# Delta rule in a hybrid encoder layer: q and k left as the convolution gives them, their norms applied as factors elsewhere

## The chip, the core and the metric

The kernel runs on one core of a Trainium2 chip. The core has TensorE (PE, matmuls and transposes into PSUM), VectorE (DVE), ScalarE (ACT), GpSimd (POOL) and SyncE (SP, which issues most of the DMAs). The metric is the time of one execution on the device in microseconds (us), lower is better. All data are float32; a large product is made of three matmuls of a rounded part and a remainder (hi x lo, lo x hi, hi x hi).

## The reference, cut to what matters

One encoder layer for two sequences, a prompt of 1024 tokens and a sample of 256, with 1024 features each: an input projection, two groups of heads side by side (four gated delta-rule heads, four differential-attention heads), an output projection, a layer norm, a SwiGLU block, a layer norm. The part that the change touches is the delta rule, which runs forward and backward in chunks:

```python
def l2norm(t, eps=1e-6):
    return t * lax.rsqrt(jnp.sum(t * t, -1, keepdims=True) + eps)

def delta_rule_chunked(q, k, v, g, beta):
    ...
    m = jnp.where(strict, jnp.einsum('bhnid,bhnjd->bhnij', kb, k) * decay, 0.0)   # kb = k * beta
    a_mat = m + jnp.eye(CHUNK, dtype=jnp.float32)
    sol = lax.linalg.triangular_solve(a_mat, rhs, ...)     # rhs: v * beta and kb * exp(gc)
    attn = jnp.einsum('bhnid,bhnjd->bhnij', q, k) * decay
    ...
    def step(state, xs):
        v_new = u_c - jnp.einsum('bhcd,bhde->bhce', w_c, state)
        o = jnp.einsum('bhcd,bhde->bhce', qd_c, state) + jnp.einsum('bhij,bhje->bhie', attn_c, v_new)
        state = state * gl_c[..., None, None] + jnp.einsum('bhcd,bhce->bhde', kd_c, v_new)

def gated_deltanet_group(qkv, z, gates, conv_w, a_log, dt_bias, norm_g):
    c = jax.nn.silu(centred_depthwise_conv(qkv, conv_w))   # 5 taps
    q, k, v = jnp.split(c, ...)
    q = l2norm(q) * (GDN_DK ** -0.5)                        # 128 features a head
    k = l2norm(k)
    ...
    o = rms_norm(o_f + o_b, norm_g) * jax.nn.silu(z)
```

## The kernel before, in words

The kernel has three stages that matter here, one behind the other. A scheduler (the program is built with a timeline model) fixes each engine's order from the order in which the code issues its instructions, with priorities; on the chip every engine works its list in that order.

**phase_a** (L592) is the input projection. `dense_T` (L175) takes up to three columns of 128 weights at a time: it loads them, splits them into hi (ACT) and lo (DVE, L163), and runs three matmuls for each of eight parts of the depth over the three token blocks (two of 512, one of 256; xh, xl are the split input; dps is the PSUM tile). After each half of a product over 512 tokens it calls `advance()` (L651), which takes one step in each of three lines of work for the delta rule: `fronts`, `blocks_` and `levels`. There are five such preparations, one for each of the four heads of the prompt and one for the sample with all of its heads. The last three columns (LAST) go through `dense_T` together; the third pair of weights, whl, borrows a buffer from the preparation.

A preparation starts from `conv_silu` (L322): five taps on DVE and a Silu on ACT, in a layout with the features on the partitions. `prep_front` (L340) transposes q, k and v on PE (nat_ps, L352) so that the tokens lie on the partitions, copies them on ACT (L355 q and k into raw, L358 v), squares them (L362), sums (L363), takes the inverse root (`rsqrt_small` L310, the power on POOL, L315), and multiplies raw by it on DVE (L371, 128x2048). `prep_group` (L385), two for each preparation with four chunks of 128 tokens each, transposes raw back (t_ps, L397), copies that on ACT into kqT (L398), writes kqT to the record rec in DRAM (L399), forms the decay factors, the products k k and k q (kq_ps, L430), and from them N, the blocks to be inverted, and more parts of the record. `invert_blocks` (L462) inverts the diagonal blocks in rows of 16 and 32 on DVE (tiles Wb, Ub, itmp, iT, iR), `spread_blocks` (L508) sends the result through DRAM into the tile UD (ublk, L512 to L517), and `invert_levels` (L526) puts the blocks together on PE: inv_ps from (UD, N) with 32x32, from (UD, Z) and (Z, UD), then the same with 64x64, with copies on ACT and DVE between them and a product with nbeta (L575) on DVE, and writes UD to rec (L578).

Two PSUM buffers of the tag tp serve all these transposes. `rope` (L750) turns the attention's q and k in the last columns' time.

**phase_b** (L1080) runs the attention and the delta rule's chunks. The attention makes 40 score tiles: s_ps (L839, L840), a maximum on DVE (L841), the exponential on ACT (L843, ap), transposes (tt_ps), the product with v, and the query steps before them (L799 to L806). Two threads of `chain` (L978) go through the chunks beside it: `chain_load` (L965) reads three tiles ld of a chunk from rec, and the first matmul of a chunk is vn_ps (L1027). `chain_finish` (L1057) squares a head's output (L1064), sums on DVE (L1066), and scales it. After that come the output projection, the layer norm and the SwiGLU block, which PE bounds and the change does not touch.

## Time and profile before

| | us |
|---|---|
| median of three runs | 1757.56 (1757.21 to 1760.45) |
| the profiled execution, its own time | 1751.05 |
| its span, first to last instruction | 1749.3 |
| projection with its preparations (phase_a) | 0 to about 509 |
| attention and chunks (phase_b) | 509 to about 801 |
| output projection to the end | 801 to 1749.3 |
| PE busy in the span | 1694.2 (97%) |
| DVE, ACT, POOL busy | 1191.9 (68%), 777.5 (44%), 213.1 (12%) |

The busy share of an engine is a mean over stages. Times in the rows are from the start of the span. The granted clock of PE is given as a share of its full speed of 2.4 GHz; 0.50 is its lower level, 1.2 GHz. The length of a matmul in the trace is from its start to its modelled end, and they overlap; how much of PE one takes is read from the distance of the starts.

### The profile page before, as it was taken

The numbers are of one execution on the slowest core, as the hardware profiler recorded it, in microseconds if no ns is written. First come the engines' busy times: TensorE is split into PE (matmuls) and PEld (weight loads), VectorE is DVE, ScalarE is ACT, GpSimd is POOL, SyncE is SP. The second block draws the span as 40 slices with busy tenths as digits, with TensorE's granted clock in tenths as the row PEclk, the third lists the DMA queues.
The fourth block names the chain that finished last, engine by engine and source line by source line (L and its number), as shares of the span: only waits on it lengthen the run. The fifth ranks groups of instructions, "written<-read, shape, count | busy, mean of one in ns | idle before, by whom it ended". The sixth has DMA issues, their size and how long they took to land.

```text
span 1749.3 us, 27337 instructions
## 1 busy us (share of the span) xinstructions
PE 1694.2 (97%) x10234; PEld 1471.2 (84%) x10234; DVE 1191.9 (68%) x2114; ACT 777.5 (44%) x1518; POOL 213.1 (12%) x197
## 2 busy tenths in 40 slices
PE   8999999999988999999999999999999999999998
PEld 8898888888867998788888888888888887888886
DVE  4635968878575589885676866556656665666696
ACT  4457486564337677775114322222222223543330
POOL 1000000000014445532330000000000000000011
PEclk9999999999988999999999999999999999999999
DMA  6234265676667996516521544333333524975541
GB/s 219 65 100 115 75 164 176 155 207 168 184 172 218 280 266 200 173 51 223 159 96 43 191 149 149 111 128 131 116 136 125 175 99 138 391 254 172 174 158 72
DMA packets 253554, 279.02 MB, mean 160 GB/s; under 512 B 47713, under 2 KB 198127, under 8 KB 252015
## 3 DMA queue, kind: packets, MB, share of 16 engines
q1 hardware_dynamic: 243519, 265.19, 48.5%
q10 hardware_dynamic: 9904, 12.10, 2.0%
q8 instruction: 80, 1.31, 0.3%
q14 instruction: 51, 0.42, 0.1%
HBM read 183.80 MB, written 93.43 MB: 158 GB/s over the span
## 4 chain that ended last, share of the span: by engine, by line
PE 54%; DMA 1%; ACT 1%; DVE 1%; issue 1%; POOLq 0%; POOL 0%; DVEq 0%; SPq 0%; ACTq 0%
PE dn_ps L1507 15%; PE gy_ps L1281 9%; PE gs_ps L1281 7%; PE gx_ps L1281 6%; PE gz_ps L1281 6%; PE om_ps L172 6%; PE gp_ps L1281 3%; DMA worw<-in_w_out_dram 1%; PE o_ps L879 1%; PE x_ps L1186 0%; ACT ap L843 0%; PE s_ps L839 0%; ACT woh L1166 0%; PE s_ps L840 0%; PE tt_ps L866 0%
## 5 line engine op out<-in xcount | busy, mean ns | idle before, releaser
L1297 ACT CAST sph<-wraw 128x512 fp32r<-128x512 f32 x92 | 57.0, 623 | 195.4 <-PE gy_ps L1281 124.4
L315 POOL TENSOR_TENSOR rs_r<-lva,mhalf 128x1 f32<-128x1 f32 x20 | 29.5, 1475 | 835.5 <-DVE lva L1143 817.1
L172 PE MATMUL dps<-xh,whi 128*128 128x512 f32 (+1 forms) x552 | 126.1, 363 | 0.0
L172 PE MATMUL dps<-xh,wlo 128*128 128x512 f32 (+1 forms) x552 | 124.5, 360 | 0.0
L172 PE MATMUL dps<-xl,whi 128*128 128x512 f32 (+1 forms) x552 | 123.4, 363 | 0.0
L1297 ACT CAST sph<-wsum 128x512 fp32r<-128x512 f32 x80 | 49.8, 622 | 156.6 <-PE gy_ps L1281 48.8
L1507 PE MATMUL dn_ps<-tth,ssh 128*128 128x512 f32 x280 | 108.9, 389 | 0.0
L1507 PE MATMUL dn_ps<-ttl,ssh 128*128 128x512 f32 x280 | 108.8, 389 | 0.0
L1507 PE MATMUL dn_ps<-tth,ssl 128*128 128x512 f32 x280 | 108.1, 389 | 0.0
L172 PEld LDWEIGHTS dps<-xh,wlo 128*128 128x128 f32 x552 | 94.8, 191 | 14.8
L172 PEld LDWEIGHTS dps<-xl,whi 128*128 128x128 f32 x552 | 94.2, 193 | 15.4
L172 PEld LDWEIGHTS dps<-xh,whi 128*128 128x128 f32 x552 | 94.5, 191 | 14.6
L841 DVE TENSOR_REDUCE ast<-s_ps 128x1 f32<-128x1024 f32 (+1 forms) x80 | 83.5, 1056 | 21.7 <-PE s_ps L840 19.6
L1298 DVE TENSOR_TENSOR spl<-wraw,sph 128x512 fp32r<-128x512 f32 x92 | 63.0, 687 | 48.2 <-PE gs_ps L1281 29.9
L334 DVE SCALAR_TENSOR_TENSOR c<-pad,cw,c 128x1024 f32<-128x1024 f32 (+1 forms) x96 | 82.1, 884 | 17.1 <-ACT c L332 16.6
L843 ACT ACTIVATE ap<-s_ps,ast 128x1024 f32<-128x1024 f32 (+1 forms) x80 | 80.0, 1001 | 29.4 <-DVE ast L841 29.1
L1298 DVE TENSOR_TENSOR spl<-wsum,sph 128x512 fp32r<-128x512 f32 x80 | 55.0, 688 | 46.6 <-issue 20.4
L1498 ACT CAST ssh<-sraw 128x640 fp32r<-128x640 f32 x77 | 56.0, 727 | 47.6 <-PE dn_ps L1507 34.3
L1499 DVE TENSOR_TENSOR ssl<-sraw,ssh 128x640 fp32r<-128x640 f32 x77 | 63.1, 820 | 16.8 <-ACT ssh L1498 13.1
L839 PE MATMUL s_ps<-akl,aq 128*128 128x512 f32 (+1 forms) x144 | 63.7, 444 | 7.7 <-ACT ap L843 7.6
L855 POOL TENSOR_TENSOR ap<-ap,ap 128x512 f32<-128x512 f32 (+2 forms) x60 | 63.0, 1069 | 64.6 <-ACT ap L852 31.6
L879 PE MATMUL o_ps<-av,tt 128*128 128x128 f32 x544 | 64.2, 275 | 0.0
(398 smaller groups left out, 4258.9 us busy)
## 6 DMA issues: line engine op xcount, KB each, us to landing
ld<-rec SPq DMA_DIRECT2D x160, 192.0 KB, 4.2
sraw<-hs SPq DMA_DIRECT2D x77, 320.0 KB, 4.3
wraw<-in_w_gate_up_dram SPq DMA_DIRECT2D x22, 1024.0 KB, 5.7
wraw<-in_w_in_dram SPq DMA_DIRECT2D x26, 512.0 KB, 4.5
wdraw<-in_w_down_dram SPq DMA_DIRECT2D x11, 1024.0 KB, 5.1
ws<-wdraw SPq DMA_DIRECT2D x11, 1024.0 KB, 3.9
traw<-ws SPq DMA_DIRECT2D x44, 256.0 KB, 4.5
araw<-dqk SPq DMA_DIRECT2D x40, 256.0 KB, 5.4
```

Of the source, the lines that this page charges most:

```text
L172: nc.tensor.matmul(out, lhsT=a(i), rhs=b(i), start=start and j == 0, stop=stop and j == len(seq) - 1)
L334: V.scalar_tensor_tensor(out=out, in0=pad[:, so + w:so + w + n], scalar=k.cw[:, w * 12 + ti:w * 12 + ti + 1], in1=out, op0=ALU.mult, op1=A ...
L839: nc.tensor.matmul(ps[:, o:o + w], lhsT=a.q[m][:, qs], rhs=a.kl[m][:, k0 + o:k0 + o + w], start=True, stop=False)
L841: V.tensor_reduce(out=st[:, m:m + 1], in_=ps, op=ALU.max, axis=AX.X, negate=True)
L843: A.activation(p, ps, AF.Exp, bias=st[:, m:m + 1], accum_out=a.s0[:, i:i + 1] if m == 0 else st[:, 2:3])
L855: nc.gpsimd.tensor_tensor(out=pr[0][:, c], in0=pr[0][:, c], in1=pr[1][:, c], op=ALU.add)
L879: nc.tensor.matmul(ps[:, j * P:(j + 1) * P], lhsT=tt[:, i, j * P:(j + 1) * P], rhs=a.v[:, v0 + i, :], start=i == 0, stop=i == NT[a.si] - 1)
L1281: m = nc.tensor.matmul(ps, lhsT=a(i), rhs=b(i), start=start and j == 0, stop=stop and j == len(seq) - 1, skip_group_check=again)
L1297: A.copy(hi, src)
L1298: V.tensor_tensor(out=lo, in0=src, in1=f32(hi), op=ALU.subtract)
L1499: V.tensor_tensor(out=lo, in0=src, in1=f32(hi), op=ALU.subtract)
L1507: nc.tensor.matmul(ps, lhsT=a[:, c], rhs=b, start=z == 0 and j == 0, stop=z == NPR - 1 and j == 2)
```

## The change

q and k stay as the convolution's Silu leaves them, features on the partitions, in one tile kqT of 128 x 2 x 1024 (two buffers in turn, by head), which is written to the record directly and is the operand of kq_ps. The transposes back and the copies behind them are gone, and so is the scaling of raw, which now holds k alone. Both are still transposed once, for their norms: the squares are read from PSUM. The inverse norm of k becomes factors: its square goes into nbeta and ekd in place, and it multiplies v on the way out of PSUM (vn, now on DVE). The inverse norm of q is kept as rq, and comes into `chain_finish` as the scale of the Square, which is now one activation for each 128 tokens with a sum of its own (eight for a prompt head, two for one of the sample), and once more in the factor of the output. The record has one axis of eight chunks rather than two of four. The flag that lets the next head's convolution go on is set behind vn; a second flag, all, is set behind the groups, and the buffers of kqT wait for it. The third weights of the last projection columns take a buffer of kqT, and the code waits for the sample's groups before it issues these columns. rope takes the other one.

```diff
 dense_T
-            hl = k.gp1.tile([P, 2, KT, P], F32R, tag=("raw", "wx")[len(W) - 2], name="whl")
+            hl = k.gp1.tile([P, 2, KT, P], F32R, tag="kqT0", name="whl")
 ...
 prep_front
-    raw = gp.tile([P, 2, 8, P], F32, tag="raw", name="raw")
+    raw = gp.tile([P, 8, P], F32, tag="raw", name="raw")
+    for s in range(2):
+        nc.sync.dma_start(out=rec[:, :, 3 + s, :], in_=kq[:, s].rearrange("p (u c) -> p u c", u=8))
     for g in range(2):
         u0 = 4 * g
-        for role in (0, 1, 2):
+        sq = gp.tile([P, 12, P], F32, tag="kq", name="sq")[:, 0:8]
+        for s in range(2):
             ps = k.pt.tile([P, 512], F32, tag="tp", name="nat_ps")
             for i in range(4):
-                nc.tensor.transpose(ps[:, i * P:(i + 1) * P], c3[role][:, (u0 + i) * P:(u0 + i + 1) * P], k.ident)
+                nc.tensor.transpose(ps[:, i * P:(i + 1) * P], kq[:, s, (u0 + i) * P:(u0 + i + 1) * P], k.ident)
             pv = ps.rearrange("p (a b) -> p a b", a=4)
-            if role < 2:
-                A.copy(raw[:, role, u0:u0 + 4], pv)
-            else:
-                vn = gp.tile([P, 4, P], F32, tag="kv", name="vn")
-                A.copy(vn, pv)
-                nc.sync.dma_start(out=k.S.rec[si][vh][g][:, :, 5, :], in_=vn)
-        sq = gp.tile([P, 12, P], F32, tag="kq", name="sq")[:, 0:8]
-        for role in range(2):
-            A.activation(sq[:, 4 * role:4 * role + 4], raw[:, role, u0:u0 + 4], AF.Square)
+            A.activation(sq[:, 4 * s:4 * s + 4], pv, AF.Square)
+            if s == 0:
+                A.copy(raw[:, u0:u0 + 4], pv)
         V.tensor_reduce(out=ss[:, :, u0:u0 + 4], in_=sq.rearrange("p (a b) c -> p a b c", a=2), op=ALU.add, axis=AX.X)
         yield
-    flag.done = True
     ...
+    inv = gp.tile([P, 8], F32, tag="l2i", name="l2i")
+    V.reciprocal(out=inv, in_=ss[:, 0])
+    nb = view(G.nbeta, o0, [[nt8, 2], [1, 8]])
+    V.tensor_tensor(out=nb, in0=nb, in1=inv.unsqueeze(1).to_broadcast([P, 2, 8]), op=ALU.mult)
+    ek = G.ekd[:, o0:o0 + 8]
+    V.tensor_tensor(out=ek, in0=ek, in1=inv, op=ALU.mult)
     rs = rsqrt_small(k, sf, 16, gp, "l2")
-    V.tensor_scalar(out=rs[:, 0:8], in0=rs[:, 0:8], scalar1=P ** -0.5, scalar2=None, op0=ALU.mult)
-    rv = raw.rearrange("p a b c -> p (a b) c")
-    V.tensor_tensor(out=rv, in0=rv, in1=rs.unsqueeze(2).to_broadcast([P, 16, P]), op=ALU.mult)
-    yield
+    V.tensor_tensor(out=inv, in0=ss[:, 0], in1=rs[:, 0:8], op=ALU.mult)
+    V.tensor_scalar(out=G.rq[:, o0:o0 + 8], in0=rs[:, 8:16], scalar1=P ** -0.5, scalar2=None, op0=ALU.mult)
+    for g in range(2):
+        ...
+            nc.tensor.transpose(ps[:, i * P:(i + 1) * P], vT[:, (u0 + i) * P:(u0 + i + 1) * P], k.ident)
+        vn = gp.tile([P, 4, P], F32, tag="kv", name="vn")
+        V.tensor_tensor(out=vn, in0=ps.rearrange("p (a b) -> p a b", a=4),
+                        in1=inv[:, u0:u0 + 4].unsqueeze(2).to_broadcast([P, 4, P]), op=ALU.mult)
+        nc.sync.dma_start(out=rec[:, u0:u0 + 4, 5, :], in_=vn)
+    flag.done = True
     yield
 ...
 prep_group
-    kqT = gp.tile([P, 4, 2, P], F32, tag="kqT", name="kqT")
-    for role in range(2):
-        ps = k.pt.tile([P, 512], F32, tag="tp", name="t_ps")
-        for i in range(4):
-            nc.tensor.transpose(ps[:, i * P:(i + 1) * P], raw[:, role, u0 + i, :], k.ident)
-        A.copy(kqT[:, :, 1 - role, :], ps.rearrange("p (a b) -> p a b", a=4))
-    nc.sync.dma_start(out=rec[:, :, 3:5, :], in_=kqT)
 ...
 invert_levels
-    for g in range(2):
-        for d, res in ((0, U), (1, Db)):
-            nc.sync.dma_start(out=k.S.rec[si][vh][g][:, :, 6 * d, :], in_=res[:, 4 * g:4 * g + 4, :])
+    for d, res in ((0, U), (1, Db)):
+        nc.sync.dma_start(out=k.S.rec[si][vh][:, :, 6 * d, :], in_=res)
 ...
 phase_a
-                            wait(flag)
-                            c3.append(conv_silu(k, 1, role, h, pad))
+                            if role == 0:
+                                wait(past, "all")
+                                out.kq = conv_out(h)
+                            elif role == 2:
+                                wait(flag)
+                                out.v = k.gp1.tile([P, 1024], F32, tag="c2", name="vT")
+                            conv_silu(k, 1, role, h, pad, (out.kq[:, 1], out.kq[:, 0], getattr(out, "v", None))[role])
 ...
             elif i == len(rest) - LAST:
+                wait(flag, "all")
                 dense_T(k, rest[i:], advance)
 ...
 rope
-        x = k.gp1.tile([P, 4, n], F32, tag=f"c{j % 2}", name="rx")
+        x = both[:, j % 2]
 ...
 chain_finish
-    A.activation(sv, o, AF.Square)
     ss = k.cf.tile([P, 8], F32, tag="css", name="css")[:, :nt]
-    V.tensor_reduce(out=ss, in_=sv, op=ALU.add, axis=AX.X)
+    rq = k.G[si].rq[:, h * nt:(h + 1) * nt]
+    for c in range(nt):
+        A.activation(sv[:, c], o[:, c], AF.Square, scale=rq[:, c:c + 1], accum_out=ss[:, c:c + 1])
     V.tensor_scalar(out=ss, in0=ss, scalar1=1.0 / P, scalar2=1e-6, op0=ALU.mult, op1=ALU.add)
     r = rsqrt_small(k, ss, nt, k.cf, "crms")
+    V.tensor_tensor(out=r, in0=r, in1=rq, op=ALU.mult)
```

The order of PE in the projection, where the preparation of the prompt's second head stands among the matmuls (dps). Before:

```order
L397 MATMUL t_ps<-identr,raw 128x128 x4
L172 MATMUL dps<-xh_153,whi 128x512
L172 MATMUL dps<-xh_283,whi 128x256
L172 MATMUL dps<-xh_153,whi 128x512
L172 MATMUL dps<-xh_283,whi 128x256
L536 MATMUL inv_ps<-UD_773,N 32x32 x32
L430 MATMUL kq_ps<-kqT 128x256 x4
L397 MATMUL t_ps<-identr,raw 128x128 x4
```

And now:

```order
L380 MATMUL nat_ps<-identr,vT 128x128 x8
L172 MATMUL dps<-xl_284,whi 128x256 x3
L172 MATMUL dps<-xh_283,wlo 128x256 x8
L172 MATMUL dps<-xh_283,whi 128x256 x8
L437 MATMUL kq_ps<-kqT 128x256 x4
L172 MATMUL dps<-xl_154,whi 128x512 x8
```

t_ps is gone, v's transposes stand by themselves behind those of q and k, and kq_ps follows without a transpose of its own.

The order of PE at the seam of the projection and the attention, where the sample's 32x32 groups (inv_ps) stand. Before:

```order
L172 MATMUL dps<-xl_284,whl 128x256 x8
L172 MATMUL dps<-xh_283,whl 128x256 x16
L839 MATMUL s_ps<-akl,aq 128x512
L840 MATMUL s_ps<-akh,aq 128x512
...
L536 MATMUL inv_ps<-UD_773,N 32x32 x32
L839 MATMUL s_ps<-akl,aq 128x512
L840 MATMUL s_ps<-akh,aq 128x512
...
L536 MATMUL inv_ps<-UD_772,Z 32x32 x8
```

And now:

```order
L172 MATMUL dps<-xl_284,whi 128x256 x8
L172 MATMUL dps<-xh_283,wlo 128x256 x4
L543 MATMUL inv_ps<-UD_775,N 32x32 x32
L172 MATMUL dps<-xh_283,wlo 128x256 x4
L172 MATMUL dps<-xh_283,whi 128x256 x8
L172 MATMUL dps<-xl_284,whi 128x256 x8
L172 MATMUL dps<-xh_283,wlo 128x256 x8
L172 MATMUL dps<-xh_283,whi 128x256 x4
L543 MATMUL inv_ps<-UD_774,Z 32x32 x8
```

The groups stood behind the first eight and twelve score matmuls; now they stand between the last 256-column matmuls of the projection, with 60 of these behind the first of them. The first vn_ps stands behind 40 score matmuls before, behind 28 now.

The order of DVE where the sample's inversion (Ub, itmp, iT from Wb) begins, near the end of the projection. Before:

```order
L163 TENSOR_TENSOR wlo<-wraw,whi 128x1024
L770 TENSOR_TENSOR rx<-rx 128x256
L163 TENSOR_TENSOR whl<-wraw,whl 128x1024
L478 COPY Ub<-Wb 128x16
L474 TENSOR_TENSOR itmp<-Wb,Ub 128x32
```

And now:

```order
L520 COPY itmp<-Ub 64x1024
L485 COPY Ub<-Wb 128x16
L481 TENSOR_TENSOR itmp<-Wb,Ub 128x32
L782 TENSOR_TENSOR rx<-rx,rcs 128x256
L482 TENSOR_REDUCE iT<-itmp 128x16
L783 TENSOR_TENSOR rx<-rx,rcs 128x256
L784 TENSOR_TENSOR rx<-rx,rcs 128x256
L481 TENSOR_TENSOR itmp<-Wb,Ub 128x32
L785 TENSOR_TENSOR rx<-rx,rcs 128x256
L163 TENSOR_TENSOR wlo<-wraw,whi 128x1024
```

It began behind the splits of the last three weights; now it begins behind head 3's last copy (the row at the top), with the three splits among its rows.

## Rows read from the trace of the kernel before

**Rows 1.** Stretches: start:end, us, busy per engine, PE clock, DMA share, GB/s.

```profile
25.00:475.00 450.00, 443.72 (x3157) 389.44 (x3156) 309.68 (x575) 253.42 (x556) 15.99 (x8) 0.98 0.51 139
324.00:336.00 12.00, 10.92 (x93) 9.38 (x94) 10.15 (x28) 6.75 (x12) 3.18 (x2) 0.72 0.48 141
400.00:410.00 10.00, 9.06 (x86) 8.06 (x87) 9.48 (x22) 5.19 (x13) 0.00 (x0) 0.66 0.66 180
525.00:550.00 25.00, 18.95 (x142) 14.42 (x141) 16.13 (x24) 17.78 (x28) 12.56 (x9) 0.70 0.49 129
675.00:725.00 50.00, 44.75 (x318) 39.22 (x317) 45.78 (x79) 43.17 (x79) 36.51 (x25) 1.00 0.60 186
```

**Rows 2.** Waits of PE, 0 to 505 us: total, times, longest.

```profile
PE inv_ps L536 <- DMA UD<-ublk: 3.7, 4, 1.5
```

**Rows 3.** PE in order of time: start, length, engine, instruction, idle before.

```profile
173.05 1.06 PE L352 MATMUL nat_ps<-identr,c 128*128 128x128 f32 x4 [1.96 <-ACT c L336]
173.76 3.38 PE L172 MATMUL dps<-xl,whi 128*128 128x512 f32 x8
...
178.84 1.98 PE L172 MATMUL dps<-xh,whi 128*128 128x512 f32 x8
```

**Rows 4.** PE in order of time, from 507 to 548 us.

```profile
507.07 2.06 PE L172 MATMUL dps<-xh,whl 128*128 128x256 f32 x16
...
517.02 3.40 PE L536 MATMUL inv_ps<-UD,N 32*32 32x32 f32 x64 [6.06 <-DMA UD<-ublk]
...
526.68 0.80 PE L839 MATMUL s_ps<-akl,aq 128*128 128x512 f32 x1
...
547.84 0.77 PE L1027 MATMUL vn_ps<-ld,ld 128*128 128x128 f32 x2 [3.66 <-DMA ld<-rec]
```

**Rows 5.** Waits of PE, 505 to 820 us.

```profile
PE s_ps L839 <- ACT ap L843: 7.6, 11, 1.4
PE inv_ps L536 <- DMA UD<-ublk: 6.1, 1, 6.1
PE vn_ps L1027 <- DMA ld<-rec: 3.7, 1, 3.7
```

**Rows 6.** One line, L397: count, length in ns (min/median/max), first, last start.

```profile
L397 PE MATMUL t_ps<-identr,raw x80: 270/272/474, 122.7 to 417.0; 128*128 128x128 f32 x80
```

**Rows 7.** PE in order of time, around 218 us.

```profile
218.15 1.03 PE L397 MATMUL t_ps<-identr,raw 128*128 128x128 f32 x8
218.94 0.37 PE L172 MATMUL dps<-xh,wlo 128*128 128x256 f32 x1
```

**Rows 8.** Two lines of DVE, L371 and L156, as in rows 6.

```profile
L371 DVE TENSOR_TENSOR raw<-raw,rs_r x5: 2276/2287/2292, 114.9 to 399.0; 128x2048 f32<-128x2048 f32 x5
...
L156 DVE TENSOR_TENSOR xl<-xps,xh x20: 684/692/692, 6.6 to 45.7; 128x512 fp32r<-128x512 f32 x20
```

**Rows 9.** DVE in order of time, the sample's inversion.

```profile
467.29 0.18 DVE L478 COPY Ub<-Wb 128x16 f32<-128x16 f32 x1
...
492.20 1.22 DVE L806 SCALAR_TENSOR_TENSOR aq<-araw,aq 64x1024 fp32r<-64x1024 f32 x1 [2.33 <-PE dps L172]
...
508.05 1.11 DVE L513 COPY itmp<-Ub 64x1024 f32<-64x1024 f32 x1
```

**Rows 10.** SP's queue in order of time, two of its issues.

```profile
458.69 1.44 SPq L469 DMA_DIRECT2D Wb<-nblk  x2
...
541.70 2.25 SPq L973 DMA_DIRECT2D ld<-rec  x5
```

**Rows 11.** ACT in order of time, around 705 us.

```profile
704.46 1.06 ACT L1064 ACTIVATE csq<-oacc 128x1024 f32<-128x1024 f32 x1
705.42 0.26 ACT L884 ACTIVATE asq<-o_ps 128x128 f32<-128x128 f32 x1
705.58 0.20 ACT L884 ACTIVATION_READ_ACCUMULATOR asq<-o_ps 128x1 f32 x1
705.67 0.58 ACT L869 COPY tt<-tt_ps 128x512 f32<-128x512 f32 x1
```

58 lines of the change are left out of this document (34 added, 24 removed).

## Prediction

> **What bounds the kernel now.** I read the table of stretches first. From 25 to 475 us, the stage of the input projection, TensorE (PE) is busy for 443.72 of 450 us, while VectorE (DVE), ScalarE (ACT) and GpSimd (POOL) have room [rows 1]. So in this stage an instruction taken off PE shortens the kernel, and one taken off ACT or DVE alone does not. The list of PE's waits says the same: before 505 us only a few have a name in the preparation of the delta rule, 3.7 us in four times for UD [rows 2] and one of 1.96 us for the convolution's c [rows 3]. A short wait costs more than itself, though. Behind that of 1.96 us, which ends at 173.05, eight matmuls of 512 columns take 3.38 us, and the next eight of that kind 1.98 us [rows 3]: the granted clock had gone from its upper level, 2.4 GHz, to the lower, 1.2 GHz. The mean granted clock is 0.72 over the 12 us from 324 and 0.66 over the 10 us from 400 [rows 1], so these two places lose (0.28 x 12) + (0.34 x 10) = 6.8 us of PE's full speed.
>
> The second place to look is the seam between projection and attention. The last projection matmuls start at 507.07; PE then does eight s_ps matmuls and sits idle for 6.06 us until 517.02, for the sample's block inverses to come back from DRAM [rows 4]. The clock falls, and the first vn_ps of the chunk chain starts only at 547.84, 38.8 us after the projection's end near 509. From 525 to 550 PE is busy for 18.95 of 25 us at a clock of 0.70 [rows 1]. The waits behind 505 us name the causes: UD 6.1 us, ld 3.7 us, and 7.6 us in eleven waits for ACT's exponentials [rows 5]. Behind 825 us nothing is touched.
>
> **The change, part by part.**
>
> *Transposes back.* 80 of them go [rows 6]. The row gives 272 ns each, but they are pipelined: eight run from 218.15 to 218.94, when the next matmul starts [rows 7], which is 0.099 us each. PE has nothing else to overlap them with, so 80 x 0.1 = 8.0 us leave PE in the bound stage. If each held PE for its whole duration it would be 80 x 0.272 = 21.8 us. I take -8.0: rows 7 show starts, not modelled ends. The Trainium skill, page "TensorE: Matmul & The Clock Gate", Part 4, gives about 275 ns for a 128x128 transpose in a kernel's context; an estimate from it would be 22 us. The row's duration agrees with that figure, its spacing of 0.1 us does not, and by the page the total below would be 14 us larger.
>
> *Copies, scaling, norms.* The copies out of the transposes and half of those out of nat_ps leave ACT, v's copies go to DVE as a multiplication, and the 128x2048 scaling leaves DVE. Five scalings of 2.287 us = 11.4 us go; ten vn of about 0.69 us (nearest row: DVE from PSUM, 128x512) = 6.9 us come [rows 8], with some 25 small operations. DVE is about where it was, ACT has less, and neither bounds: 0. The vn step now waits for the norm on POOL; PE does not wait behind it unless both PSUM buffers of the transposes are still held. That would be a wait of the kind at 173 us, 1.96 + 1.4 us for each; a gain is possible too, if the present ones vanish. I take 0, with +10 and -10 as ends (the last is the 6.8 us of clock and the 3.7 us of waits).
>
> *The seam.* Taking the sample's q and k from kqT0, and holding the last projection columns until its preparation is written out, sets the sample's inversion on DVE earlier: directly behind head 3's, not behind the split of the last weights. Before, DVE began the sample at 467.29, 8.6 us behind the issue of the read that brings its N blocks back (458.69 [rows 10]), and ended it at 509.16 [rows 9], 41.9 us. In the new order the preparation stands about a column of the projection earlier, 24 x (0.23 + 0.23 + 0.12) = 13.9 us, and 8 us of transposes are gone: it begins near 467.3 - 21.9 = 445.4 and ends, with the same length, at 487.3. The 41.9 us hold steps of others, too; of attention's two query steps among them the one at 492.20, with its wait of 2.33 us for PE [rows 9], now stands behind the end: 1.2 + 2.3 = 3.5 us less, so 484 to 487. From its end to the arrival of UD it took 517.0 - 509.2 = 7.9 us: UD is there at 492 to 495. In the new order PE reaches the 32x32 groups inside the projection, with 60 matmuls of 256 columns still to come; these run at 0.12 us (16 in 2.06 [rows 4]), 7.2 us. The projection's end moves to about 509 - 8 + 4 = 505, so PE gets there near 494. UD is there just in time, or a us late. What leaves the seam: the wait, 6.1 us; the 32x32 groups, which with four s_ps fill 517.02 to 526.68, at 0.42 us for an s_ps (3.38 / 8 [rows 3]) 9.7 - 1.7 = 8.0 us; and 12 of the 40 s_ps matmuls that stood before the first vn_ps (28 now), 12 x 0.42 = 5.0. Together 19.1. Given back: the groups at full clock inside the projection, half of 8.0 = 4.0, and the 12 s_ps later, 12 x 0.23 = 2.7. Net -12.4. ACT is busy for 17.78 of 25 us from 525 to 550 [rows 1], and the exponentials and the ld transfers, issued from 541.70 on [rows 10], may set the pace instead; with a us of waiting for UD I take -9, from 0 (UD late) to -12.4.
>
> *The output's norm.* For each prompt head one Square of 1024 columns and a DVE reduction become eight squares of 128 columns with a sum. The nearest row is that of the attention's norm: such a square with its read takes 0.25 us (705.42 to 705.67), the large Square 0.96 us (704.46 to 705.42) [rows 11]. Eight make 2.0, so +1.0 on ACT for a head, +4.2 for four; by the full durations, 0.26 + 0.20 for each, 3.7 - 1.05, +10.6. From 675 to 725 ACT has 6.8 of 50 us free and PE 5.3 [rows 1]. I take +1.5, from 0 to +10.6. The Trainium skill, page "ScalarE: Activation LUTs", section "What ACT_TABLE_LOAD costs", speaks against this split: each activation pays a fixed 186 ns and 93 ns for a pointer operand. An estimate from it is 0.29 us for a small one, +1.4 us for a head, 5.6 us in all, where the row gives 4.2; the sum would hardly differ.
>
> *DMA.* The record is written with shorter rows for k and q and the same bytes, the UD record in two transfers, not four; ld reads what it read. On SP's queue that is 2 issues fewer for a preparation: 0.
>
> *Sum.* -8.0 + 0 - 9 + 1.5 = -15.5 us. The profiled run took 1751.05 us (span 1749.3), so 1735.5 for a run like it. The median of the runs shown, 1757.56, is 6.5 us above it, and a change in PE's work moves both: **1742 us**.
>
> **The rivals.**
> - *Only the transposes pay.* The sample's inversion is still late, because DVE waits in order behind the weights' split or the N blocks' trip; PE then stands in the projection rather than behind it, and the first vn_ps comes as late as before. For it: the inversion hangs on two trips through DRAM and on DVE's order. Against: by the estimate UD comes within a us or two of PE. -8.0 + 1.5: 1751 us.
> - *More than I count.* Each transpose held PE for its 0.272 us, -13.8 more, 1728; or the waits of the preparation and their half clock, 10 us, go with the new order, 1732. The Trainium skill's page on TensorE, cited above, would lead to the first. For it: the four transposes and matmuls at other places overlap in ways that rows 7 don't show. Against: their spacing.
> - *Given back inside the projection.* Three new short waits with their stretches at the lower clock, 3 x (1.96 + 1.4) = 10.2 us, and the seam half as good: -8.0 + 1.5 - 4.5 + 10.2 = -0.8, 1757 us, no change that can be measured.
> - *Slower.* k's tile in PSUM is now read twice by ACT, by the square and by the copy, before its buffer is free, and PE's next eight transposes stand behind it: two groups in each of five preparations. At the price of a wait with its slow stretch, 1.96 + 1.4 = 3.4 us, five such waits eat the whole gain of 15.5, from there on it decides; with eight it is 8 x 3.4 - 15.5 = +11.7, 1769 us. Against: ACT is also freed of forty copies.
>
> **How the numbers follow.** The forecast (1736 to 1748) gets 0.48, only the transposes 0.20, more than I count 0.15, given back 0.09, slower 0.08. The range 1728 to 1753 holds the first two and most of the third. A measurement of this kernel tells about 0.2%, 3.5 us, from no change: faster 0.83, same 0.09, slower 0.08.
>
> **What would show it.** In the profile after, the projection's last matmuls start near 503, four to six us earlier than now, with the 32x32 groups inside them and no wait for UD there; the first vn_ps stands near 525 to 530; from 500 to 550 PE's busy time rises and its clock with it. The list of PE's waits before the seam should hold no more than 6 us of nat_ps and UD. In 675 to 725 ACT's busy time rises by 4 us or so and PE's waits for ap by under 2. I am wrong if PE waits for inv_ps inside the projection (first rival), if nat_ps or kq_ps shows waits in every preparation (slower), or if s_ps waits for ap in the seam take all that UD's wait gave.

## The result and the profile after

The changed kernel takes **1766.66 us** (median of 4 runs, 1762.97 to 1767.78), the kernel before beside it 1757.38: a ratio of 1.0057, 95% interval 1.0040 to 1.0074. It is slower by 9 to 10 us where 15.5 us of gain were forecast, and outside the range of 1728 to 1753. The profiled run after took 1762.97 us, its span is 1761.2; that of before was 1749.3. All medians here and below leave out two executions in a slow state, one of e5 (1991.83 us) and one of e13 (2391.0), whose mean granted clocks were 0.79 and 0.65.

Where the 11.9 us between the two spans arise is best seen by comparing the starts of the same matmuls in the two traces. Each column is one kernel's start less that of before, in us; the kernels e1, e6, e13 to e16 are the experiments below.

| PE starts | before | after | e1 | e6 | e13 | e14 | e15 | e16 |
|---|---|---|---|---|---|---|---|---|
| matmul 1440 of the projection | 439.5 | -5.9 | -5.5 | +3.6 | -10.7 | -1.2 | +8.1 | -13.5 |
| first s_ps (the projection's end) | 509.0 | +6.2 | +8.0 | +4.8 | -6.3 | -2.9 | +7.8 | -9.0 |
| first vn_ps (the chunk chain) | 547.8 | -10.0 | -7.8 | -24.0 | -22.4 | +4.4 | -11.4 | -25.1 |
| vn_ps 132 of 160 | 718.6 | +1.2 | +9.2 | -3.0 | -9.7 | +9.4 | +5.2 | -9.0 |
| om_ps 160 (the output projection) | 843.7 | 0.0 | +8.9 | -1.4 | -9.1 | +10.5 | +9.1 | -8.7 |
| last gs_ps (feed-forward, first half) | 1462.2 | +4.0 | +8.9 | -0.7 | -9.1 | +10.8 | +9.7 | -4.7 |
| dn_ps 1152 (its end) | 1740.1 | +11.8 | +11.0 | +2.0 | -6.4 | +11.0 | +10.3 | +2.7 |

Each column is one execution, and a cell can be off by several us. The trace of before (1751.05 us) is some 6 us below that kernel's median. Kernels that share an order of PE differ as well: e2, e3 and e9 have the order of before in the projection and stand at +1.8, -5.5 and +1.1 at matmul 1440, and after and e1 have one order throughout and are 8 us apart at vn_ps 132. The step from om_ps to the end does repeat: the three kernels whose tiles are moved by 160 bytes (after, e2, e16) lose 10.1 to 11.8 us there, the fourteen others 0.3 to 3.4.

The column "after" has three parts: the projection gains 5.9 us and then loses 12; the seam gains 16 and the chunk stage gives the 10 us of lead back; and from 844 us on, where the diff changes no line, 11.8 us are lost.

**The stretches.** This is the table of stretches of the kernel after, with the columns of [rows 1] and the same five windows.

```profile
25.00:475.00 450.00, 437.81 (x3119) 384.75 (x3118) 319.10 (x635) 242.29 (x525) 16.31 (x12) 0.98 0.52 143
324.00:336.00 12.00, 12.00 (x136) 10.37 (x135) 11.70 (x29) 2.87 (x7) 0.00 (x0) 0.89 0.24 66
400.00:410.00 10.00, 10.00 (x73) 8.39 (x72) 9.43 (x17) 5.05 (x13) 0.00 (x0) 1.00 0.48 145
525.00:550.00 25.00, 22.65 (x121) 18.48 (x120) 16.55 (x24) 19.82 (x32) 14.17 (x14) 0.67 0.93 287
675.00:725.00 50.00, 41.96 (x283) 37.60 (x283) 39.57 (x72) 44.36 (x120) 34.88 (x24) 0.93 0.56 170
```

The two windows that cost clock before are better (0.72 to 0.89, 0.66 to 1.00), but the lower clock stands at other places now: its mean over the 450 us is 0.98 in both kernels. Up to the first s_ps PE loses 13.7 us to it, where before it lost 10.2 (half of the time that it runs at 0.50). PE is idle for 12.2 us of the 450 instead of 6.3, and in 675 to 725 its busy time fell by 2.8 us while its clock went from 1.00 to 0.93.

**The projection.** First PE's list of waits from 0 to 505 us (total, times, longest), then PE in order of time.

```profile
PE inv_ps L543 <- DMA UD<-ublk: 13.7, 3, 6.2
...
PE nat_ps L358 <- ACT kqT L336: 0.7, 1, 0.7
PE nat_ps L358 <- ACT sq L360: 0.3, 1, 0.3
```

```profile
235.43 2.08 PE L543 MATMUL inv_ps<-UD,N 32*32 32x32 f32 x64 [2.83 <-DMA UD<-ublk]
317.26 3.43 PE L543 MATMUL inv_ps<-UD,N 32*32 32x32 f32 x64 [6.17 <-DMA UD<-ublk]
499.93 3.40 PE L543 MATMUL inv_ps<-UD,N 32*32 32x32 f32 x64 [4.68 <-DMA UD<-ublk]
515.17 0.40 PE L856 MATMUL s_ps<-akl,aq 128*128 128x512 f32 x1
537.86 0.77 PE L1044 MATMUL vn_ps<-ld,ld 128*128 128x128 f32 x2 [0.54 <-DMA ld<-rec]
```

The waits for UD inside the projection grew from 3.7 us in four [rows 2] to 13.7 us in three, the last of them that for the sample, which before stood behind the projection. Behind the two long ones the 64 groups take 3.4 us where at the upper clock they take 2.08. PE came to the sample's groups at 499.93 - 4.68 = 495.25, near the forecast (494); UD did not. The next rows are SP's queue at that place, and behind them the same two steps in the kernel before.

```profile
488.36 0.62 SPq L519 DMA_DIRECT2D ublk<-Ub  x1
489.12 1.06 SPq L521 DMA_DIRECT2D ublk<-itmp  x1
490.27 2.31 SPq L812 DMA_DIRECT2D araw<-dqk  x2
492.69 0.60 SPq L816 DMA_DIRECT2D araw<-dqk  x1
493.34 5.96 SPq L524 DMA_DIRECT2D UD<-ublk  x8
```

```profile
509.98 0.89 SPq L514 DMA_DIRECT2D ublk<-itmp  x1
512.67 4.26 SPq L517 DMA_DIRECT2D UD<-ublk  x8
```

Behind the write of the inverted blocks stand three reads of attention's queries, and only from 493.34 on the eight reads of UD, which take 6 us of the queue. From the write's issue the first of these is 4.2 us away, where it was 2.7 before, and the eight took 4.3 us. From the end of DVE's last copy, at 489.1, to the start of PE's groups are 10.8 us, where it was 7.9 before.

**The chunk stage.** This is PE's list of waits from 505 to 820 us, to be read against [rows 5].

```profile
PE s_ps L856 <- ACT ap L860: 11.6, 10, 2.2
PE ks_ps L1027 <- ACT oT L918: 3.9, 1, 3.9
...
PE tt_ps L883 <- DVE cz L1094: 2.4, 1, 2.4
```

The waits for UD and most of that for ld are gone. In their place are 4.0 us more for ACT's exponentials and two waits for results that stand at the end of a head. From the first vn_ps to om_ps 160 the kernel takes 305.9 us for 295.8: PE is idle for 21.3 us of it and not for 16.1, the lower clock costs 7.0 us and not 3.8, and the 12 score matmuls that stood ahead of the first vn_ps are done here (some 2.7 us). ACT in order of time shows what it does there: the squares of the output's norm.

```profile
696.09 0.39 ACT L1084 ACTIVATE csq<-oacc,rq 128x128 f32<-128x128 f32 x1
696.38 0.19 ACT L1084 ACTIVATION_READ_ACCUMULATOR csq<-oacc,rq 128x1 f32 x1
696.48 0.39 ACT L1084 ACTIVATE csq<-oacc,rq 128x128 f32<-128x128 f32 x1
```

One square with its read takes 0.39 us from start to start, not the 0.25 of the nearest row [rows 11].

**The feed-forward part.** PE in order of time, in the kernel before and then in the kernel after, at one weight tile.

```profile
1103.26 1.07 PE L1281 MATMUL gz_ps<-B11l,sph 128*128 128x512 f32 x4
1104.17 1.07 PE L1281 MATMUL gz_ps<-B11h,sph 128*128 128x512 f32 x4
```

```profile
1105.00 1.09 PE L1300 MATMUL gz_ps<-B11l,sph 128*128 128x512 f32 x4
1105.93 1.10 PE L1300 MATMUL gz_ps<-B11h,sph 128*128 128x512 f32 x4
```

Four matmuls of 512 columns take 0.91 us before and 0.93 after, at full clock and with no wait. The shapes, the instructions and their order are the same. It is 2%, but on thousands of matmuls.

### The profile page after: what moved, and what is told of

Its sections match the earlier page's. It is cut to its first block, busy times and chain, and to the rows that moved or that the text cites. A ratio compares the mean times of both kernels' runs of the same rounds, so it can differ in the third digit from the quotient of the medians.

```text
span 1761.2 us, 27233 instructions
## 1 busy us (share of the span) xinstructions
PE 1698.4 (96%) x10154; PEld 1467.7 (83%) x10154; DVE 1190.3 (68%) x2139; ACT 772.5 (44%) x1556; POOL 213.5 (12%) x197
## 4 chain that ended last, share of the span: by engine, by line
PE 61%; DVE 2%; DMA 2%; ACT 1%; issue 1%; POOL 0%; POOLq 0%; SPq 0%; DVEq 0%; ACTq 0%
PE dn_ps L1526 15%; PE gy_ps L1300 9%; PE gs_ps L1300 7%; PE gx_ps L1300 6%; PE om_ps L172 6%; PE gz_ps L1300 6%; PE gp_ps L1300 3%; PE o_ps L896 2%; PE tt_ps L883 1%; PE s_ps L856 1%; PE s_ps L857 1%; DMA araw<-dqk 1%; PE ks_ps L1027 1%; PE vn_ps L1044 1%; PE qs_ps L1034 1%
## 5 line engine op out<-in xcount | busy, mean ns | idle before, releaser
L172 PE MATMUL dps<-xh,wlo 128*128 128x512 f32 (+1 forms) x552 | 128.6, 367 | 0.0
L172 PEld LDWEIGHTS dps<-xh,whi 128*128 128x128 f32 x552 | 95.8, 195 | 15.5
L1518 DVE TENSOR_TENSOR ssl<-sraw,ssh 128x640 fp32r<-128x640 f32 x77 | 62.9, 819 | 18.8 <-ACT ssh L1517 15.2
L1517 ACT CAST tth<-traw 128x512 fp32r<-128x512 f32 x56 | 34.3, 620 | 69.7 <-PE dn_ps L1526 67.2
```

The costliest lines, as they stand in the source:

```text
L172: nc.tensor.matmul(out, lhsT=a(i), rhs=b(i), start=start and j == 0, stop=stop and j == len(seq) - 1)
L1517: A.copy(hi, src)
L1518: V.tensor_tensor(out=lo, in0=src, in1=f32(hi), op=ALU.subtract)
```

## Experiments

All ratios are against runs of the kernel before on the same chip. The medians of before there lie between 1755.65 and 1757.71. Most differences between two experiments below are taken from the medians; where they were timed on different chips the ratios are the better measure.

| kernel | what | us | ratio and interval |
|---|---|---|---|
| after | the change | 1766.66 | 1.0057 (1.0040 to 1.0074) |
| e1_pad | after, its constants padded to 256 bytes | 1759.65 | 1.0018 (1.0005 to 1.0031) |
| e2_before_160 | before, 160 unused bytes | 1766.24 | 1.0059 (1.0037 to 1.0080) |
| e3_before_64 | before, 64 unused bytes | 1756.54 | 0.9997 (0.9985 to 1.0009) |
| e5_ud_act | e1, UD read on ACT's queue | 1758.77 | 1.0024 (1.0003 to 1.0044) |
| e6_transposes | e1, 80 transposes put back | 1753.24 | 0.9989 (0.9974 to 1.0004) |
| e7_last2 | e1, two columns held back, not three | 1755.61 | 1.0003 (0.9989 to 1.0017) |
| e12_later | e1, the 32x32 groups a step later | 1750.99 | 0.9971 (0.9958 to 0.9984) |
| e13_last2_later | e7 and e12 together | 1739.53 | 0.9904 (0.9883 to 0.9925) |
| e18_e13_again | e13 once more | 1743.13 | 0.9929 (0.9908 to 0.9951) |
| e14_before_edits | before with e13's two edits | 1765.78 | 1.0040 (1.0022 to 1.0058) |
| e15_last2_later_tr | e13, 80 transposes put back | 1756.31 | 0.9992 (0.9975 to 1.0010) |
| e16_last2_later_nopad | e13 without the pad | 1753.25 | 0.9974 (0.9956 to 0.9992) |
| e9_before_squares | before, eight squares for one | 1762.18 | 1.0040 (1.0027 to 1.0054) |
| e4_one_square | e1, one square for eight | 1765.60 | 1.0053 (1.0033 to 1.0074) |
| e10_last2_one | e7, one square for eight | 1762.06 | 1.0028 (1.0014 to 1.0041) |
| e17_no_pointer | e13, squares without the factor | 1745.89 | 0.9940 (0.9922 to 0.9959) |

### The place of the tiles: e1, e2, e3

The change makes two new constants, rq0 and rq1, 32 and 128 bytes a partition. By the addresses of the built programs, the tiles allocated behind them lie 160 bytes further (the streamed operand tth of dn_ps at 28800 for 28640, B00h of gx_ps at 67712 for 67552), while the weight tiles sph and spl, at 215008, do not move. e1 pads the constants so that the shift is 256 bytes; e2 and e3 leave the change out and put unused bytes into the kernel before.

```
e1:  -    G.rq = cp.tile([P, n8 // 2], F32, name=f"rq{si}")
     +    G.rq = cp.tile([P, 32], F32, name=f"rq{si}")[:, 0:n8 // 2]
e2:  egt{si} = cp.tile([P, n8 + 40 * si], ...)[:, 0:n8]   (was [P, n8])
e3:  egt{si} = cp.tile([P, n8 + 16 * si], ...)[:, 0:n8]
```

> The changed kernel with its two new small tiles rq widened to 128 bytes a partition each, so that everything behind them moves by 256 bytes instead of 160; every engine's order is that of the changed kernel. Address theory: the 512-column matmuls of the SwiGLU block whose streamed operand stood on a 64-byte boundary (starts 0.233 us apart, 0.227 before) are back at 0.227; from the first down-projection matmul to the end and from 933 us on some 9 to 10 us go, so about 1757 median, level with the kernel before. Rival (the difference behind 930 us is chance of the runs, the waits for UD in the projection make the whole loss): no change against the changed kernel, about 1766.

> The kernel before with 160 unused bytes a partition put where the changed kernel has rq; the same instructions in the same order on every engine. Address theory: 9 to 10 us slower than before, 1767, with 0.233 us between the starts of dn_ps<-ttl,ssh and of gx_ps and gz_ps from the B tiles, gs_ps 0.002 us closer, and the projection as it was. Rival: 1757, as before.

> The kernel before with 64 unused bytes in the same place: the tiles keep their place within 64 bytes, not within 128. Address theory, if 64 bytes are what counts: as before, 1757. If the place within 128 or 256 bytes counts: between 1757 and 1767. Rival: 1757.

The order of the instructions on every engine is that of after (e1) and of before (e2, e3). e2 alone, with nothing of the change, is as slow as the changed kernel: 1.0059. e1 takes 7.0 us off the change. The same rows of gz_ps as above, first of e1, then of e2:

```profile
1088.63 1.07 PE L1300 MATMUL gz_ps<-B11l,sph 128*128 128x512 f32 x4
1089.54 1.07 PE L1300 MATMUL gz_ps<-B11h,sph 128*128 128x512 f32 x4
```

```profile
1084.77 1.09 PE L1281 MATMUL gz_ps<-B11l,sph 128*128 128x512 f32 x4
1085.70 1.10 PE L1281 MATMUL gz_ps<-B11h,sph 128*128 128x512 f32 x4
```

The median time between two starts, worked out from all such matmuls of each trace, in ns:

| matmuls | before | after | e1 (256) | e2 (160) | e3 (64) |
|---|---|---|---|---|---|
| dn_ps<-tth,ssh 512 columns | 227 | 233 | 227 | 233 | 227 |
| dn_ps<-ttl,ssh 512 columns | 226 | 233 | 226 | 233 | 232 |
| gz_ps<-B11h,sph 512 columns | 227 | 236 | 227 | 236 | 228 |
| gz_ps<-B11l,sph 512 columns | 227 | 232 | 227 | 232 | 234 |
| gs_ps<-xsl,sph 256 columns | 120 | 117 | 120 | 117 | 117 |
| om_ps<-woh,oh 512 columns | 227 | 227 | 227 | 227 | 227 |

After a shift of 256 bytes the spacing is the old one, after 160 it is 5 to 9 ns longer for these groups of 512 columns and 3 ns shorter for gs_ps, after 64 it is longer for some and shorter for others, and the sum is no change (0.9997). om_ps keeps its spacing in all; by the built programs its tiles do not move. gy_ps reads the same weights sph against the tiles T3h and T3l, which do not move either, and keeps 227 ns in all five. So it is the groups whose streamed tile moves that change. From om_ps to the end after loses 11.8 us and e2 10.1, against 2.1 in e1 and 2.3 in e3. So the place of the tiles costs 7 to 10 us of the result, and it has nothing to do with what the change computes. What decides (the streamed tile's place by itself, or against that of the weights) was not tried.

### The waits for UD: e5, e7, e12

With the pad the change is still 2 to 3 us slower than before, so the forecast fails apart from the tiles' place, too. The theory is the wait for UD: in the new order PE reaches the 32x32 groups before the blocks are back. The rival is ACT, which sets the pace of the chunk stage whatever the seam does.

```
e5:  -            nc.sync.dma_start(out=diag(k, t, b), ...)
     +            nc.scalar.dma_start(out=diag(k, t, b), ...)
e7:  -LAST = 3            +LAST = 2
     -                wait(flag, "all")     (before the last columns)
e12:                  spread_blocks(k, si, vh)
     +                yield
                      yield from invert_levels(k, si, vh, N, k.G[si])
```

> As e1_pad, but the eight reads that bring UD back from DRAM are issued on ACT's queue and not on SP's, where they stood behind up to three reads of araw, writes of the record and loads of weights. The scheduler leaves the inverse groups at the same places in PE's order. Theory that SP's queue makes UD late and that these waits, with their stretches at the lower clock, took what the transposes gave: PE's waits for UD before 515 us fall from 13.7 us to under 6, the first s_ps starts near 508 instead of 515, the total is about 1753, 5 or more below e1_pad. Rival (the inversion on DVE itself is late, the queue adds little): waits for UD of 10 us or more remain, the total within 2 us of e1_pad.

> As e1_pad, but the last columns go through the projection two at a time and not three, so that no third weights take kqT's buffer and nothing is held until the sample's preparation is written out. Theory that this hold is what sets the sample's inversion and the record's transfers against each other at the seam: UD's wait of 4.7 us at 500 goes or halves, and the total is 3 to 6 us below e1_pad. Rival (the place of the inverse groups in the projection comes from the earlier preparation, not from the hold): the wait at 500 and the total stay within 2 us of e1_pad.

> As e1_pad, with one more step of the preparation between the issue of UD's trip through DRAM and the inverse groups on PE. The scheduler puts the 32x32 groups of the prompt's second and third head 44 and 25 projection matmuls later in PE's order, the sample's 22. Theory that these groups were put ahead of their data (13.4 us of waits for UD before 517 us, then half clock): the waits fall under 7 us, the projection ends 5 us or more before e1_pad's 517, the total is 3 to 6 us below e1_pad, about 1755. Rival (the trip is late by more, or the waits move to others): waits of 10 us or more, the total within 2 us of e1_pad, 1760.

e5 moves the reads past SP's queue and gains nothing that can be measured: 1758.77 against 1759.65, by the ratios 1.0024 against 1.0018. Its waits before 512 us, then the sample's write, reads and groups in order of time:

```profile
PE nat_ps L358 <- ACT raw L362: 5.0, 1, 5.0
PE xps L152 <- DMA xn<-in_x_prompt_dram: 4.7, 1, 4.7
PE inv_ps L543 <- DMA UD<-ublk: 4.5, 1, 4.5
```

```profile
495.86 1.08 SPq L521 DMA_DIRECT2D ublk<-itmp  x1
499.27 7.38 ACTq L524 DMA_DIRECT2D UD<-ublk  x8
507.21 3.40 PE L543 MATMUL inv_ps<-UD,N 32*32 32x32 f32 x64 [4.50 <-DMA UD<-ublk]
```

The waits for UD fell from 13.4 us in e1 to 4.5, but the reads wait for the write in ACT's own stream now, and a copy out of nat_ps stands behind them: 5.0 us that were not there. The order of PE is not quite that of e1 either: from 231 us on it differs in some 550 places. The trip of the sample's blocks is no shorter without the three reads in its way: 11.4 us from the end of DVE's copy (495.83) to PE's groups. e7 saves 4 us, with 8.8 us of waits for UD in two. e12, which lets PE do one step of the projection between the issue of the reads and the groups, saves 8 to 9 us, with 6.0 us of waits for UD in two, and is 0.3% faster than the kernel before. So the groups did stand ahead of their data in PE's order, as the theory says.

### Both edits, and what they are worth alone: e13, e18, e14

> The edits of e7_last2 and e12_later together. If the hold at the last columns and the early place of the inverse groups are separate costs, the gains add: 7 to 10 us below e1_pad, 1750 to 1753, below the kernel before. If they are one cost: as the better of the two. Whatever the start of the chunk chain gains, the theory that the stage up to the output projection is not bound by that start says that the output projection begins no more than 3 us earlier than the projection's end explains.

> e13_last2_later once more, unchanged, to stand beside e17 on one chip and to say how well its time repeats. Theory A (its gain is its own): 1737 to 1744, ratio 0.987 to 0.993. Rival B (six runs caught it low): 1745 to 1750, ratio 0.993 to 0.997, in which case what e15 and e16 lost against it shrinks by as much.

> The kernel before with the two edits of e13_last2_later (two columns held back instead of three, and the 32x32 groups one step later), and nothing of the change. Theory A: e13's gain is the change's own, set free by the two edits. The kernel before has no wait for UD worth more than 3.7 us in the projection, and its sample stands behind the projection's end either way, so that the wait of 6 us there stays: 1752 to 1760, ratio 0.997 to 1.002. Rival B: the two edits alone are the gain, whatever the change does: 1738 to 1745, ratio about 0.990 to 0.993. Between the two, 0.994 to 0.997, each holds a part.

e13 takes 1739.53 us and, run once more, 1743.13: 0.7 to 1.0% faster than before and the fastest kernel here. That is more than the sum of the two gains that its expectation allowed (1750 to 1753). Its wait for UD before 505 us, then PE in order of time at the sample's groups, then SP's queue there:

```profile
PE inv_ps L543 <- DMA UD<-ublk: 1.1, 2, 0.9
```

```profile
492.08 2.08 PE L543 MATMUL inv_ps<-UD,N 32*32 32x32 f32 x64 [0.85 <-DMA UD<-ublk]
...
502.70 0.40 PE L856 MATMUL s_ps<-akl,aq 128*128 128x512 f32 x1
```

```profile
481.43 0.49 SPq L519 DMA_DIRECT2D ublk<-Ub  x1
482.58 0.46 SPq L521 DMA_DIRECT2D ublk<-itmp  x1
486.59 0.46 SPq L812 DMA_DIRECT2D araw<-dqk  x1
487.10 4.68 SPq L524 DMA_DIRECT2D UD<-ublk  x8
```

This is the seam that the prediction drew for the change itself: UD a us late, the groups at the upper clock, the projection's end at 502.7, the first vn_ps at 525.5. Its time is the predicted 1742, but not by the predicted terms: of the 22.4 us by which its first vn_ps leads, 13.3 are gone at om_ps 160, and the trace as a whole is 6.3 us below that of before, not 15.5. That the medians meet the forecast is partly luck. e14, the same edits on the kernel before, is 7 to 8.5 us slower than before: rival B is out, the edits alone gain nothing, and e13's gain needs the change. Theory A had said 1752 to 1760 here and did not foresee this loss; e14's trace shows 11.3 us of waits for UD before 520 us and 46.2 us from the first s_ps to the first vn_ps, for 38.9 before.

### The transposes: e6, e15

```
e6, e15, at the start of prep_group (results unused):
+    for role in range(2):
+        ps = k.pt.tile([P, 512], F32, tag="tp", name="t_ps")
+        for i in range(4):
+            nc.tensor.transpose(ps[:, i * P:(i + 1) * P], raw[:, u0 + i, :], k.ident)
```

> As e1_pad, with 80 transposes of raw put back where the kernel before had them (their results are not used, and no copy follows). If a transpose costs 0.1 us of a bound PE, the last projection column comes 8 us later and the total is 8 us above e1_pad, about 1767. If each holds PE for its 0.272 us: 22 us later. Rival (PE waits in the preparation anyway, so the transposes fill its waits): the total within 3 us of e1_pad. The scheduler also moves other work when they are put back (12 score matmuls stand before the first vn_ps, not 28), so the total can differ by some us either way; the place of the projection's middle columns in time is the better measure.

> e13_last2_later with the 80 transposes of raw put back (their results are not used). Theory A: where PE no longer waits for UD, the 8 to 9 us that the transposes cost at column #1440 reach the end, at least in part: 1743 to 1749, which is 4 to 9 us above e13. Rival B: as with e6 against e1, what PE loses before the seam it finds again, because DVE and the round trip through DRAM set the pace there: within 3 us of e13, 1737 to 1743. The places of the transposes shift the order of the levels a little (24 s_ps before the first vn_ps, 28 in e13), which is worth about 1 us either way.

At matmul 1440 of the projection e6 stands 3.6 + 5.5 = 9.1 us behind e1, which looks like 0.11 us for each of 80 transposes. But 160 more 32x32 matmuls of inv_ps stand ahead of that place in e6 (5.2 us, an estimate from 64 in 2.08 us), and PE is idle for 3.9 us less there, so the two nearly cancel. A cleaner measure takes idle time and lower clock out. From the first dps to matmul 1440 the kernel before takes 392.6 us, of which PE is idle for 5.0 and loses 10.2 to the lower clock: 377.4 are left. After takes 384.9, less 10.0 and 6.8: 368.1. Up to there both lists of PE hold the same matmuls but for the 80 transposes, so these take 9.3 us, 0.12 each. Other traces agree: 376.7 to 378.1 in e2, e3, e9 and e14, 367.3 to 369.2 in the others without the transposes. e6 has 381.9, less 5.2 for its 160 matmuls 376.7, which is 8.8 above e1 (367.9). That is near the predicted 8.0. At the end, though, e6 is 5 to 6 us faster than e1. PE's list of waits before 512 us holds, for e6:

```profile
PE kq_ps L441 <- DVE e_b L449: 3.7, 1, 3.7
PE inv_ps L547 <- DMA UD<-ublk: 1.7, 1, 1.7
```

With the transposes PE waits 1.7 us for UD, not 13.4. Its first s_ps stands 3.2 us ahead of that of e1; the order at the seam differs too (12 score matmuls before the first vn_ps, not 28), and how much of the total each is worth is not shown. In e13, where there is little left to wait for, the same 80 transposes cost 11 to 17 us, more than theory A allowed. 18.8 us are there by matmul 1440 and 14.1 at the projection's end. Of the 18.8, about 9 are the transposes and 2 are 64 matmuls of inv_ps that stand ahead of that place in e15 alone; the rest is idle time (2.5 us more) and lower clock (5.9 us more). The waits before 505 us:

```profile
PE inv_ps L547 <- DMA UD<-ublk: 6.1, 4, 2.9
...
PE nat_ps L358 <- ACT kqT L336: 4.0, 2, 3.6
```

So the transposes' own price is right, and it can't be read from a total: moving 9 us of PE work moves waits and lower clock of the same size, in either direction.

### The tiles' place once more: e16

```
e16, on e13:  the line of e1 undone
```

> e13_last2_later without the widened tile: the same order, the tiles behind the new constants 160 bytes further, as in the change itself. Theory A: the place of the streamed operands costs the feed-forward part what it cost the kernel before when that was moved by 160 bytes (8.5 us of median there), less where it was the change itself (7 us): 1746 to 1749, ratio 0.994 to 0.996; gz_ps and dn_ps groups of 512 columns 0.232 to 0.236 us apart instead of 0.227. Rival B: the place matters only through the waits that e13 no longer has: within 3 us of e13.

Ratio 0.9974 for 0.9904 and 0.9929 of e13's two measurements: 8 to 12 us. In the table at the top e16 is 8.7 us ahead of before at om_ps 160 and 2.7 us behind it at the end: 11.4 us lost, 2.7 in e13. Theory A had the mechanism and was a few us short of the size.

### The squares: e9, e4, e10, e17

```
e9 (on before):  -    A.activation(sv, o, AF.Square)   and V.tensor_reduce(...)
                 +    for c in range(nt):
                 +        A.activation(sv[:, c], ..., AF.Square, accum_out=ss[:, c:c + 1])
e4 (on e1), e10 (on e7):  one Square, one V.tensor_reduce and two small products with rq again
e17 (on e13):    the eight squares without scale=rq, and the two small products
```

> The kernel before with the eight squares with a sum in place of one Square and a DVE reduction in chain_finish, and nothing else. Theory that the small squares cost ACT's time in the stage of 683 to 713 us: ACT's busy time from 675 to 725 rises by 4 us, the total by 2 to 5 us, about 1761. Rival (ACT has room there, the reduction leaves DVE): within 1 us of 1757.6.

> As e1_pad, and in chain_finish one Square of the whole head and one DVE reduction as before, with two small multiplications by rq behind it, instead of eight squares with a sum. Theory that the small squares cost the stage of 683 to 713 us its 5 us on ACT: vn_ps number 132 some 5 us earlier than in e1_pad, the output projection's first matmuls earlier by up to 5, the total 3 to 5 us below e1_pad, about 1753. Rival (the last stage before the output projection waits for something else that comes at a fixed time): the stage is shorter, the output projection starts as in e1_pad, and the total is within 1 us of it.

> As e7_last2, with one Square and a DVE reduction for each head in chain_finish in place of the eight squares with a sum, and two small multiplications; every engine's order is that of e7_last2 up to the first finished head (near 680 us). Theory that the eight squares cost the time (the kernel before lost about 5 us by them): 3 to 5 us below e7_last2, about 1751. Rival (which engine's order the scheduler finds behind 680 us decides, and not the squares, as e4_one_square was 6 us above e1_pad): the same as e7_last2 or above it, 1755 to 1761.

> e13_last2_later with the squares of the output's norm taken without the factor of rows as their scale (two small multiplications of the sums on DVE in its place): a square with its read should take 0.29 us between starts, as in e9, instead of 0.38, so ACT loses 4 x 8 x 0.09 = 2.9 us for the prompt's heads. Theory A (ACT sets the pace of the chunk stage): 1 to 3 us below e13. Rival B (the order that the planner makes from it decides): behind the first finished head some 4285 lines of PE's list differ, as they did in e4 and e10, which lost 6 us by it: 3 to 8 us above e13.

e9 puts the eight squares into the kernel before and costs 6.1 us by the medians (4.7 to 9.5 by the ratio's interval). Taking them out of the change should then give as much back; e4 and e10 lose 4 to 6 us instead. In each the planner also makes another order of the chunk stage from the changed costs. By name of tile and shape, PE's order in the traces differs from that of its partner in 248 places for e9, 358 for e4, 322 for e10 and 266 for e17 (a count with buffer numbers, as in the expectation of e17, is far larger and says little). So none of the four, e9 included, has the squares alone. e17 shortens a square, as ACT's rows show:

```profile
L1084 ACT ACTIVATE csq<-oacc x40: 294/312/359, 604.3 to 759.0; 128x128 f32<-128x128 f32 x40
```

against those of the kernel after:

```profile
L1084 ACT ACTIVATE csq<-oacc,rq x40: 385/394/452, 619.9 to 769.8; 128x128 f32<-128x128 f32 x40
```

It ends at 1745.89 beside 1743.13 of e18; the intervals overlap, and neither theory is borne out. The squares' own price, told apart from the order that comes with them, stays open.

## Why the prediction was wrong

Point by point, by its own steps:

- **Transposes, -8.0: right.** They take 9.3 us of PE when idle time and lower clock are left out; the 5.9 us at matmul 1440 of one trace are what a start 1.8 us later, 5.0 us more of idle time and 3.4 us less of lower clock left of it. The estimate from 272 ns each (21.8 us), and with it the rival of 1728 us, is not what the rows show. The Trainium skill, page "TensorE: Matmul & The Clock Gate", Part 4, has 275 ns for a transpose; the row's duration agrees, but what 80 of them take from PE in sequence is 9 us.
- **Copies, scaling, norms, 0: right as to PE.** The waits for nat_ps in the projection are 1.0 us in two; the rival "slower" (by these waits) did not occur.
- **The seam, -9: failed at the arrival of UD.** The step was "From its end to the arrival of UD it took 517.0 - 509.2 = 7.9 us: UD is there at 492 to 495." PE's side was right to a us, partly by luck: two waits that the forecast did not have, 2.83 and 6.17 us, lie ahead of that point. DVE ended at 489.1, not 484 to 487, and the trip took 10.8 us, not 7.9. I had treated the trip as a constant, and it is none: from the end of DVE's copy to PE's groups it is 6.1 us in e12, 9.5 in e13, 9.1 in e18 and 11.4 in e5. In the new order three other reads stand between the write and the reads of UD on SP's queue, but e5, which takes the reads past them, is no shorter, so what makes the trip long stays open. The same happened at two earlier heads (the 2.83 and 6.17 us), where I had looked for no change: there, too, PE's order now has the groups ahead of their data, and e12, which puts them later, takes 8 to 9 us off. This is the rival "given back inside the projection", three new short waits, to which I gave 0.09. Its 10.2 us, half clock included, were somewhat small: the waits alone grew by 13.7 - 3.7 = 10.0 us, and what the lower clock costs up to the first s_ps by 3.4.
- **What leaves the seam reaches the end: failed.** The first vn_ps came 10.0 us earlier (22.4 in e13), and at vn_ps 132 that lead was gone (9.7 left in e13). The prediction let it go through the chunk stage untouched. All kernels with the change lose 10 to 23 us against the kernel before between the first vn_ps and om_ps. The prediction counted 2.7 of these, for the score matmuls that come later; the rest is idle time and lower clock of PE, in the trace after 5.2 and 3.2 us more than before. That ACT, by the waits for ap and the ends of heads, sets the pace there, so that a chain that begins earlier runs into them earlier, fits the list of waits, but no experiment has shown it.
- **The output's norm, +1.5: too small on ACT, open in time.** A square took 0.38 us, not 0.25: the row I took has no factor of rows as its scale, and even without one (e9, e17) a square takes 0.29. Eight are 3.1 us for 1.0, so ACT has +2.0 a head, not +1.0; from 675 to 725 us, though, its busy time rose by 1.2 us and not by the 4 of the prediction. e9 makes it 6.1 us of time, inside the bounds of 0 to 10.6, but e4 and e10 point the other way, and the order changed in all three. The Trainium skill, page "ScalarE: Activation LUTs", section "What ACT_TABLE_LOAD costs", gives 186 ns and 0.833 ns an element, and 93 ns for a pointer operand. An estimate from these figures is 293 ns for 128 elements without a pointer operand and 386 with one; the shortest rows, 294 ns in e17 and 385 in after, agree with it, and the medians are 312 and 394. My 0.29 us from that page is too small to hold all three terms.
- **"Behind 825 us nothing is touched": failed**, and at 7 to 10 us it alone turns a small loss into the measured one. No line behind 825 us is touched, but two constants of 160 bytes in all move the tiles there. The prediction had no term for it.

Together: without the tiles' place the result would have been about 1760, by e1: the transposes' gain, eaten by the waits for UD, and a seam that the chunk stage gives back. With the padded constants, two columns held back and the groups one step later (e13) the forecast time of 1742 is reached, though not by the forecast's terms.

## What to carry over

A step that is moved must be timed on both sides: when the engine arrives, and when the data does, in the new order, for a trip through DRAM is no constant; a short delay of the consumer can be worth as much as the work removed. Compare the addresses of the tiles before and after a change as one compares the order of the instructions, and time a padded version beside it, lest a new constant be taken for the cost of an idea. A lead at the start of a stage need not reach its end: look at both. And read a price from one trace only after taking out its idle time and its lower clock, beside a second trace with the same order.

## What the runs showed of the hardware

The same matmuls, in the same order and with nothing to wait for, start 0.227 or 0.232 to 0.236 us apart for 512 columns, and 0.120 or 0.117 for 256, by where their streamed tile lies in SBUF: moved by 160 bytes those of 512 columns are slower, by 256 bytes not at all, by 64 bytes in part. In this kernel that was 0.4 to 0.6% of the time.

A 128x128 transpose lasts 0.27 us in the trace but takes 0.10 us of PE in a row of eight, and 80 of them take 9.3 us.

A square of 128 columns on ACT with a factor for each row as its scale takes 0.38 us with its read, without that factor 0.29.
